# Value products of a decoder layer's attention: one product per key block over up to 384 queries, from transposed probabilities kept for a whole group

## The chip, the cores and the metric

The kernel runs on one core of one Trainium2 chip. The metric is device time in microseconds for one execution of the whole layer; the time before is the median of three runs.

## The reference

One layer of a decoder for 512 positions of width 1024, one batch. After a modulated RMSNorm and one input projection there are two head groups, each of 8 heads of 64 that share 2 key-value heads (below: g = 0, 1; r = 0..3 counts the heads within one g). Group A is sliding-window attention; group B adds three branches, each weighted by a gate:

```python
# A: 128-query blocks, window 128: each block sees its own and the previous key block
o_a = banded_gqa(qa, ka, v_a, 128, rel_bias[:, :8], sinks)
# B: compressed (31 key blocks), selected (here all 8 blocks of 64 fit top-16), window 512
p_c = masked_softmax(q @ k_cmp, c_end <= t);   o_cmp = p_c @ v_cmp
p_s = masked_softmax(q @ k_sel + bias, s <= t); o_sel = p_s @ v_sel
o_win = banded_gqa(qb, k_win, v_win, 512, bias_b, None)
o_b = gb[0] * o_cmp + gb[1] * o_sel + gb[2] * o_win
y = concat(o_a * silu(z_a), o_b * silu(z_b));  out = x + gate * (y @ w_out)
```

With 512 positions, the selected and the window branch are both full causal attention with their own keys and values.

## The kernel before

All matrix products of weights run three times in a split form (a high and a low part of each fp32 number); they stand at L293/L294 (first projection), L484 (`unit_nat`) and L494 (`unit_col`). The attention products on transposed probabilities run in plain fp32.

The attention is cut into slots. A slot is (kind, r, br, i): head r of both g, branch br, query block i of 128. For kind "a" there are 16 slots, each with one or two key blocks. For kind "b" each r has seven: (3, 0), which does query block 0 of both token branches at once, then (1, 1..3) for the selected branch and (2, 1..3) for the window branch, with i + 1 key blocks. `run` (L985) is a pipeline written by hand: in step t it transposes slot t-2, scales slot t-1, computes the scores of slot t, and after the last query block of a group computes the value products of all the slots of that group. Between these it advances a stream (`gen12`) of projection work by an estimated number of microseconds (`per`). A scheduler then orders the instructions of each engine by these priorities and its own estimates; `block()` keeps the TensorE instructions of scores, transposes and value products in their written order, but lets other TensorE work stand between them.

`slot_trans` (L932) transposes the probabilities `pp`/`pa` on TensorE into a PSUM tile `pt`, and ScalarE copies that, query order reversed, to an SBUF tile `ptT` (L942 for one or two key blocks, L952 once per g for three or four). `slot_pv` (L956) multiplies: for one slot, one key block and one g, a stationary 128x64 block of values (`va`, `vs`, `vw`) and a moving 128x128 block of `ptT`, into the 64 rows of g in the PSUM tile `po`. So a head has 14 products in group A, 22 in the selected branch (with 2 + 2 for query block 0) and 18 in the window branch. After the window branch two more products (L974) add the compressed branch from `vc`, of which the 32 rows of r are used, and `PTc`. Then `make_y` (L825) multiplies `po` by the SiLU gate and splits it into `yh` and `yl` for the output projection. The pool `t2` has 38 tiles of 128x512, 16 of which hold `hh` and `hl`, the split input of all projections.

Of the kernel before, what the change touches and what calls it, by code (L numbers as in the profile page):

```python
# [9 lines left out]
F32 = mybir.dt.float32  # L10
# [18 lines left out]
NT2 = 38  # L29
# [52 lines left out]
def hybrid_layer_kernel(ctx, tc, A, out):  # L82
# [42 lines left out]
    hh = [T2(F32R, f"hh{k}") for k in range(8)]  # L125
    hl = [T2(F32R, f"hl{k}") for k in range(8)]
# [485 lines left out]
    def cmp_mlp():  # L612
# [38 lines left out]
        for g in range(2):  # L651
            vc[g] = mp.tile([128, HD], F32, name=f"vc{g}")
            ACT.activation(vc[g], pv[:, 64 * g:64 * g + 64], AF.Copy)
# [278 lines left out]
    def slot_trans(sl):  # L932
        kind, r, br, i = sl["id"]
        P, w = sl["P"], sl["w"]
        nb = w // 128
        if nb <= 2:
            T = T2(F32, "ptT").rearrange("p (g b q) -> p g b q", g=2, b=2)
            pt = PT()
            for g in range(2):
                for b in range(nb):  # L940
                    PE.transpose(pt[:, (nb * g + b) * 128:(nb * g + b + 1) * 128], P[:, g, b * 128:(b + 1) * 128], ident)  # L941
            ACT.copy(T[:, :, 0:nb, :], rev(pt[:, 0:2 * nb * 128].rearrange("p (g b q) -> p g b q", g=2, b=nb)))  # L942
            sl["T"] = [T[:, g] for g in range(2)]
        else:
            sl["T"] = []
            for g in range(2):
                T = T2(F32, "ptT").rearrange("p (b q) -> p b q", b=4)
                sl["T"].append(T)
                pt = PT()
                for b in range(nb):  # L950
                    PE.transpose(pt[:, b * 128:(b + 1) * 128], P[:, g, b * 128:(b + 1) * 128], ident)  # L951
                ACT.copy(T[:, 0:nb, :], rev(pt[:, 0:nb * 128].rearrange("p (b q) -> p b q", b=nb)))  # L952
# [3 lines left out]
    def slot_pv(sl):  # L956
        kind, r, br, i = sl["id"]
# [3 lines left out]
        v = (va, vs, vw, None)[br]  # L961
        nb, j0 = sl["w"] // 128, sl["lo"] // 128
        last = kind == "a"
        first_of = kind == "a" or br == 3
        for b in range(nb):
            for g in range(2):
                vb = (vs, vw)[b][:, 0] if br == 3 else v[:, j0 + b]
                PE.matmul(o[64 * g:64 * g + 64, 128 * i:128 * i + 128], vb[:, 64 * g:64 * g + 64],  # L968
                          sl["T"][g][:, b, :], start=first_of and b == 0, stop=last and b == nb - 1,
                          skip_group_check=True)  # L970
        if i == NB - 1 and br in (0, 2):
            if kind == "b":
                for g in range(2):
                    PE.matmul(o[64 * g:64 * g + 64, :], vc[g][32 * r:32 * r + 32, :],  # L974
                              PTc[g][32 * r:32 * r + 32, :], start=False, stop=True, skip_group_check=True)
# [9 lines left out]
    def run(slots, stream):  # L985

        n = len(slots)
        group = []
        for t in range(n + 3):
            per = PER_A if t < 16 else PER_B[t - 16 >= PER_B[2]]  # L990
            if t < n:
                kind, r, br, i = slots[t]["id"]
                if kind == "a" and i == 0 and r >= 2:
                    load_bias_b(r - 2)
            if 0 <= t - 2 < n:
# [7 lines left out]
            stream.adv(per / 2)  # L1003
            if 0 <= t - 3 < n:
                group.append(slots[t - 3])
                kind, r, br, i = slots[t - 3]["id"]
                if i == NB - 1:
                    with block():
                        for sl in group:
                            slot_pv(sl)  # L1010
                    group = []
                    if kind == "b" and br == 2 and r + 2 < 4:
                        load_bias_b(r + 2)
            stream.adv(per / 2)
# [106 lines left out]
```

## Time and profile before

| | |
|---|---|
| time, median of 3 runs | 313.88 us (313.81 to 314.51) |
| the profiled execution's own time | 314.01 us |
| its span, first to last instruction | 312.2 us |
| TensorE matmuls busy | 304.6 us (98%) |
| VectorE / ScalarE busy | 237.0 us (76%) / 196.9 us (63%) |
| value products at L968, with L974 | 30.2 us of TensorE |
| granted TensorE clock | 1.00 throughout |

Each engine runs its own queue in order, and "busy" is the union of the durations of its instructions. Matmuls overlap each other in time, so what a matmul costs is read from the distance between starts, not from its duration. Each fp32 product of the program appears as two matmul records: 18 products of the window branch are a timeline row "x36".

### The profile page before, as it was taken

To read this page: it belongs to the slowest core of one execution; us is meant where nothing else is said; L and a number is where in the kernel's file an instruction comes from. 1 tells how busy PE (TensorE), PEld (TensorE's weight loads), DVE (VectorE), ACT (ScalarE), POOL (GpSimd) and SP (SyncE) were. 2 spreads that over 40 slices of the span, in tenths; PEclk is the share of its full clock that TensorE was granted. 3 is DMA by queue.
4 is the path that set the end of the run, shared out by engine and by line. 5 is a ranking of instruction groups with operands and counts; after the bars stand their busy time and mean duration, and the time that the engine had idled before them with its cause. 6 is when DMAs were issued, how large, how long until landed. Compare 5 with 4: busy or idle time off the path is not lost.

```text
span 312.2 us, 5975 instructions
## 1 busy us (share of the span) xinstructions
PE 304.6 (98%) x2175; PEld 255.7 (82%) x2175; DVE 237.0 (76%) x668; ACT 196.9 (63%) x477; POOL 4.9 (2%) x21
## 2 busy tenths in 40 slices
PE   8899999999999999999999999999999999999995
PEld 4577778889989889999976887888788788788885
DVE  4779998999896378886989899898678787645221
ACT  5765467677877575978958757877577586502200
POOL 1000000000000000000000000000000000000000
PEclk9999999999999999999999999999999999999999
DMA  7999969623250591141132440337003031352301
GB/s 286 377 398 309 417 217 284 172 87 122 70 156 16 166 347 63 35 136 34 37 134 63 128 181 2 127 90 258 2 0 136 0 138 67 103 202 93 110 34 67
DMA packets 27420, 44.21 MB, mean 142 GB/s; under 512 B 1712, under 2 KB 19408, under 8 KB 27392
## 3 DMA queue, kind: packets, MB, share of 16 engines
q1 hardware_dynamic: 27392, 43.84, 42.0%
q8 instruction: 17, 0.28, 0.4%
q14 instruction: 11, 0.09, 0.1%
HBM read 41.70 MB, written 2.14 MB: 140 GB/s over the span
## 4 chain that ended last, share of the span: by engine, by line
PE 85%; DVE 9%; DMA 2%; ACT 1%; issue 1%; SPq 0%; DVEq 0%
PE pj L494 30%; PE pj L484 10%; PE s L893 8%; PE sq L293 8%; PE po L968 7%; PE pt L951 4%; PE pt L941 4%; PE skv L294 4%; DVE wl L176 2%; PE s L620 2%; DMA xf<-in_xn 2%; PE pt L541 1%; PE po L974 1%; DVE qn L532 1%; DVE qc L536 1%
## 5 line engine op out<-in xcount | busy, mean ns | idle before, releaser
L175 ACT ACTIVATE wh<-raw 128x512 fp32r<-128x512 f32 (+1 forms) x52 | 31.2, 630 | 27.8 <-PE pj L494 27.7
L176 DVE TENSOR_TENSOR wl<-raw,wh 128x512 fp32r<-128x512 f32 (+1 forms) x52 | 35.1, 692 | 7.4 <-ACT wh L175 5.6
L484 PE MATMUL pj<-wh,hl 128*128 128x256 f32 (+1 forms) x128 | 36.9, 288 | 0.0
L484 PE MATMUL pj<-wh,hh 128*128 128x256 f32 (+1 forms) x128 | 36.8, 289 | 0.0
L484 PE MATMUL pj<-wl,hh 128*128 128x256 f32 (+1 forms) x128 | 36.5, 286 | 0.2
L905 ACT ACTIVATE pp<-pp,nm 128x256 f32<-128x256 f32 (+2 forms) x48 | 29.2, 610 | 6.3 <-DVE nm L898 6.2
L494 PE MATMUL pj<-hh,wh 128*128 128x512 f32 x80 | 32.8, 410 | 0.0
L494 PE MATMUL pj<-hl,wh 128*128 128x512 f32 x80 | 31.8, 397 | 0.0
L494 PE MATMUL pj<-hh,wl 128*128 128x512 f32 x80 | 31.7, 397 | 0.0
L898 DVE CUSTOM_DVE_ANT_0 pp<-s,bias 128x256 f32<-128x256 f32 (+2 forms) x48 | 25.4, 550 | 4.9 <-PE s L893 4.8
L494 PE MATMUL pj<-yl,wh 128*128 128x512 f32 (+1 forms) x72 | 26.7, 370 | 0.0
L494 PE MATMUL pj<-yh,wl 128*128 128x512 f32 (+1 forms) x72 | 26.6, 370 | 0.0
L494 PE MATMUL pj<-yh,wh 128*128 128x512 f32 (+1 forms) x72 | 26.3, 370 | 0.0
L484 PEld LDWEIGHTS pj<-wl,hh 128*128 128x128 f32 x128 | 24.1, 189 | 0.7 <-DVE wl L176 0.7
L484 PEld LDWEIGHTS pj<-wh,hl 128*128 128x128 f32 x128 | 24.1, 188 | 0.2 <-issue 0.2
L484 PEld LDWEIGHTS pj<-wh,hh 128*128 128x128 f32 x128 | 24.0, 188 | 0.0
L1047 DVE SCALAR_TENSOR_TENSOR fin<-pj,gate,xr 128x512 f32<-128x512 f32 (+1 forms) x9 | 6.2, 692 | 22.7 <-PE pj L494 22.7
L893 PE MATMUL s<-kTb,qs 128*128 128x256 f32 (+2 forms) x96 | 23.0, 358 | 0.0
L926 DVE TENSOR_SCALAR pp<-pp,rr,grev 128x256 f32<-128x256 f32 (+2 forms) x48 | 21.1, 474 | 0.4
L898 DVE CUSTOM_DVE_ANT_0 pa<-s,bias,nsink 128x256 f32<-128x256 f32 (+1 forms) x32 | 14.3, 449 | 9.4 <-PE s L893 8.4
L952 ACT COPY ptT<-pt 128x384 f32<-128x384 f32 (+1 forms) x32 | 15.7, 531 | 6.3 <-PE pt L951 5.1
L942 ACT COPY ptT<-pt 128x512 f32<-128x512 f32 (+1 forms) x28 | 15.4, 550 | 6.2 <-PE pt L941 6.0
(249 smaller groups left out, 718.8 us busy)
## 6 DMA issues: line engine op xcount, KB each, us to landing
ada_ring<-in_w_ada_ss SPq DMA_DIRECT2D x16, 512.0 KB, 8.7
raw<-in_w_cmp SPq DMA_DIRECT2D x8, 512.0 KB, 4.7
raw<-in_w_gate SPq DMA_DIRECT2D x8, 512.0 KB, 4.1
raw<-in_w_o SPq DMA_DIRECT2D x8, 512.0 KB, 5.2
wst_ring<-in_w_qkv_a SPq DMA_DIRECT2D x8, 384.0 KB, 9.3
bias<-line_d SPq DMA_DIRECT2D x8, 256.0 KB, 4.3
raw<-in_w_q_b SPq DMA_DIRECT2D x4, 512.0 KB, 5.9
raw<-in_w_z_a SPq DMA_DIRECT2D x4, 512.0 KB, 7.5
```

The source lines that it names most:

```text
L175: ACT.activation(wh, src, AF.Copy)
L176: DVE.tensor_tensor(wl, src, wh.bitcast(F32), op=OP.subtract)
L293: PE.matmul(pj_q[tb], lt, w[:, 0:512], start=f, stop=l, skip_group_check=True)
L484: PE.matmul(bank[:, t * n:(t + 1) * n], h[:, tb * 128:(tb + 1) * 128], w[:, k % 2, :], start=k == 0 and m == 0, stop=k == 7 and m == 2)
L494: PE.matmul(bank, w, h[:, cols], start=k == 0 and m == 0, stop=k == 7 and m == 2)
L893: PE.matmul(ps, qs[h][:, 128 * i:128 * i + 128], k[:, hl_, lo:lo + n], start=hl_ == 0, stop=hl_ == 1)
L898: DVE.tensor_tensor_reduce(out=P[:, g, 0:w], in0=ps[:, 0:w], in1=bt, scale=1.0, scalar=init, op0=OP.add, op1=OP.min, accum_out=nm[:, g:g + 1])
L905: ACT.activation(P[:, g, 0:e], P[:, g, 0:e], AF.Exp, bias=nm[:, g:g + 1], scale=-1.0, accum_out=dn[:, g:g + 1])
L926: DVE.tensor_scalar(v, v, rr[:, g:g + 1], gates[:, g, br:br + 1], op0=OP.mult, op1=OP.mult)
L942: ACT.copy(T[:, :, 0:nb, :], rev(pt[:, 0:2 * nb * 128].rearrange("p (g b q) -> p g b q", g=2, b=nb)))
L952: ACT.copy(T[:, 0:nb, :], rev(pt[:, 0:nb * 128].rearrange("p (b q) -> p b q", b=nb)))
L968: PE.matmul(o[64 * g:64 * g + 64, 128 * i:128 * i + 128], vb[:, 64 * g:64 * g + 64], sl["T"][g][:, b, :], start=first_of and b == 0, stop= ...
```

## The change

Three edits belong together.

The transposed probabilities of a whole group stay in one tile: `TTb` (128 keys x 2 g x 4 key blocks x 384 queries) for kind "b", and `TT0`/`TT1` (seven blocks of 128) in turn for kind "a". Query block 0 of kind "b" stays in its own `ptT`. `slot_trans` copies into the right part.

`group_pv` takes the place of `slot_pv`. It goes by key block j: for kind "b" the queries from max(128, 128 j) to 512, so 384, 384, 256 and 128 columns; for kind "a" 256, 256, 256 and 128. A head has 8 products in group A and 10 in each branch of group B. `run` now calls it at the beginning of a step, ahead of the next slot's transposes and scores, where before it stood after them and half of the stream's share. The load of the bias for head r + 2 moves with it.

The compressed values `vc` become a tile of 128 rows x 4 x 64, zero except for rows 32 r to 32 r + 32 of column block r, filled by two memsets on GpSimd and eight copies on ScalarE in place of two; the product uses all 128 rows of `vc` and `PTc`.

To make room, `hh` and `hl` move from `t2` into two tiles of eight parts, and `t2` has 22 tiles.

```diff
-NT2 = 38
+NT2 = 22
...
-    hh = [T2(F32R, f"hh{k}") for k in range(8)]
-    hl = [T2(F32R, f"hl{k}") for k in range(8)]
+    hhl = [con.tile([128, 8, S], F32R, name=name) for name in ("hh", "hl")]
+    hh, hl = ([t[:, k] for k in range(8)] for t in hhl)
...
-            vc[g] = mp.tile([128, HD], F32, name=f"vc{g}")
-            ACT.activation(vc[g], pv[:, 64 * g:64 * g + 64], AF.Copy)
+            vc[g] = mp.tile([128, 4, HD], F32, name=f"vc{g}")
+            POOL.memset(vc[g], 0.0)
+            for r in range(4):
+                own = slice(32 * r, 32 * r + 32)
+                ACT.activation(vc[g][own, r, :], pv[own, 64 * g:64 * g + 64], AF.Copy)
...
+        if br == 3:
+            T = zeroth[r] = T2(F32, "ptT").rearrange("p (g b q) -> p g b q", g=2, b=2)
+        elif kind == "a":
+            T = turned(kind, r, br)[:, :, i + sl["lo"] // 128:][:, :, 0:nb]
+        else:
+            T = turned(kind, r, br)[:, :, 0:nb, 128 * i - 128:128 * i]
...
+    def turned(kind, r, br):
+        key = "b" if kind == "b" else r % 2
+        if key not in TT:
+            TT[key] = mp.tile([128, 2, NB, 384] if kind == "b" else [128, 2, 7, 128], F32, name=f"TT{key}")
+        return TT[key]
...
+    def group_pv(kind, r, br):
...
+        if kind == "a":
+            for j in range(NB):
+                nq = min(2, NB - j)
+                todo.append((j, 128 * j, 128 * nq, [T[:, g, 2 * j:2 * j + nq] for g in range(2)], j == 0, j == NB - 1))
+        else:
+            todo.append((0, 0, 128, [zeroth[r][:, g, br - 1] for g in range(2)], br == 1, False))
+            for j in range(NB):
+                q0 = max(128, 128 * j)
+                todo.append((j, q0, S - q0, [T[:, g, j, q0 - 128:384] for g in range(2)], False, False))
+        for j, q0, n, src, begin, end in todo:
             for g in range(2):
-                vb = (vs, vw)[b][:, 0] if br == 3 else v[:, j0 + b]
-                PE.matmul(o[64 * g:64 * g + 64, 128 * i:128 * i + 128], vb[:, 64 * g:64 * g + 64],
-                          sl["T"][g][:, b, :], start=first_of and b == 0, stop=last and b == nb - 1,
+                PE.matmul(o[64 * g:64 * g + 64, q0:q0 + n], v[:, j, 64 * g:64 * g + 64], src[g], start=begin, stop=end,
                           skip_group_check=True)
...
-                    PE.matmul(o[64 * g:64 * g + 64, :], vc[g][32 * r:32 * r + 32, :],
-                              PTc[g][32 * r:32 * r + 32, :], start=False, stop=True, skip_group_check=True)
+                    PE.matmul(o[64 * g:64 * g + 64, :], vc[g][:, r, :], PTc[g], start=False, stop=True,
+                              skip_group_check=True)
...
+            if 0 <= t - 3 < n:
+                kind, r, br, i = slots[t - 3]["id"]
+                if i == NB - 1:
+                    with block():
+                        group_pv(kind, r, br)
+                    if kind == "b" and br == 2 and r + 2 < 4:
+                        load_bias_b(r + 2)
             if 0 <= t - 2 < n:
...
-            stream.adv(per / 2)
-            if 0 <= t - 3 < n:
-                group.append(slots[t - 3])
...
-                            slot_pv(sl)
...
-            stream.adv(per / 2)
+            stream.adv(per)
```

TensorE, the value products of head r = 1 of group A, first before and then changed (`va`: values; `pa`: probabilities; `csh`, `csT`, `csTv`: the small network that makes the compressed keys and values; `kT`, `qs`: keys and queries of the scores; `wh`, `wl`, `hh`, `hl`: projections):

```order
L893 MATMUL s<-kT_672,qs_892 128x256 x2
L968 MATMUL po<-ptT,va 64x128 x14
L941 MATMUL pt<-first,pa 128x128 x4
L893 MATMUL s<-kT_670,qs_876 128x256 x2
L762 MATMUL pt<-gsig,rest 128x96
```

```order
L896 MATMUL s<-kT_658,qs_878 128x256 x2
L988 MATMUL po<-TT_1182,va 64x256
L634 MATMUL pt<-first,csh 128x128 x2
L988 MATMUL po<-TT_1182,va 64x256 x4
L645 MATMUL s<-rest,csT 64x64 x2
L988 MATMUL po<-TT_1182,va 64x256
L988 MATMUL po<-TT_1182,va 64x128
L649 MATMUL s<-rest,csTv 128x64
L988 MATMUL po<-TT_1182,va 64x128
L484 MATMUL pj<-wh,hh 128x280
L649 MATMUL s<-rest,csTv 128x64 x3
```

One unbroken run of products has become three pieces with transposes and 128-column products of the small network between them.

TensorE, the selected branch of head r = 1 of group B, before and then changed (`pp`: probabilities; L951 and L955 are the transposes of slots with three or four key blocks):

```order
L951 MATMUL pt<-first,pp 128x128 x4
L893 MATMUL s<-kTb_671,qs_1953 128x384 x2
L893 MATMUL s<-kTb_673,qs_1967 128x384 x2
L941 MATMUL pt<-first,pp 128x128 x4
L494 MATMUL pj<-hh_79,wh 128x512
L893 MATMUL s<-kTb_671,qs_1953 128x512 x2
L893 MATMUL s<-kTb_673,qs_1967 128x512 x2
L494 MATMUL pj<-hl_87,wh 128x512
L494 MATMUL pj<-hh_79,wl 128x512
L968 MATMUL po<-ptT,vs 64x128 x2
L968 MATMUL po<-ptT,vw 64x128 x2
L968 MATMUL po<-ptT,vs 64x128 x18
```

```order
L955 MATMUL pt<-first,pp 128x128 x8
L896 MATMUL s<-kTb_657,qs_1917 128x384 x2
L896 MATMUL s<-kTb_659,qs_1931 128x384 x2
L988 MATMUL po<-ptT,vs 64x128 x2
L494 MATMUL pj<-hh,wl 128x512
L988 MATMUL po<-TTb,vs 64x384 x4
L988 MATMUL po<-TTb,vs 64x256 x2
L988 MATMUL po<-TTb,vs 64x128 x2
L949 MATMUL pt<-first,pp 128x128 x4
L896 MATMUL s<-kTb_657,qs_1917 128x512 x2
L896 MATMUL s<-kTb_659,qs_1931 128x512 x2
```

The products now stand four scores behind the group's last transposes; before, four transposes, eight scores and three projection matmuls lay between.

TensorE at the end of the attention, head r = 3, window branch, before and then changed (`yh`, `yl`: the output projection's input; `ptc`, `vc`: the compressed branch):

```order
L951 MATMUL pt<-first,pp 128x128 x6
L494 MATMUL pj<-yh_2659,wl 128x512
L951 MATMUL pt<-first,pp 128x128 x8
L968 MATMUL po<-ptT,vw 64x128 x18
L974 MATMUL po<-ptc_2580,vc_1452 64x512
L974 MATMUL po<-ptc_2590,vc_1454 64x512
```

```order
L955 MATMUL pt<-first,pp 128x128 x4
L494 MATMUL pj<-yh_2586,wh 128x512
L494 MATMUL pj<-yl_2587,wh 128x512
L955 MATMUL pt<-first,pp 128x128 x4
L988 MATMUL po<-ptT,vw 64x128 x2
L988 MATMUL po<-TTb,vw 64x384 x4
L988 MATMUL po<-TTb,vw 64x256 x2
L988 MATMUL po<-TTb,vw 64x128 x2
L993 MATMUL po<-ptc_2515,vc_1426 64x512
L993 MATMUL po<-ptc_2525,vc_1432 64x512
```

The products follow the last transposes at once in both; before they began with the two earlier query blocks, now the third product already reads all three.

More of the change, by code (lines that the diff above doesn't have):

```diff
@@ L941, in slot_trans @@
                     PE.transpose(pt[:, (nb * g + b) * 128:(nb * g + b + 1) * 128], P[:, g, b * 128:(b + 1) * 128], ident)
-            ACT.copy(T[:, :, 0:nb, :], rev(pt[:, 0:2 * nb * 128].rearrange("p (g b q) -> p g b q", g=2, b=nb)))
-            sl["T"] = [T[:, g] for g in range(2)]
+            ACT.copy(T, rev(pt[:, 0:2 * nb * 128].rearrange("p (g b q) -> p g b q", g=2, b=nb)))
         else:
-            sl["T"] = []
             for g in range(2):
-                T = T2(F32, "ptT").rearrange("p (b q) -> p b q", b=4)
-                sl["T"].append(T)
                 pt = PT()
@@ L951, in slot_trans @@
                     PE.transpose(pt[:, b * 128:(b + 1) * 128], P[:, g, b * 128:(b + 1) * 128], ident)
-                ACT.copy(T[:, 0:nb, :], rev(pt[:, 0:nb * 128].rearrange("p (b q) -> p b q", b=nb)))
+                ACT.copy(T[:, g], rev(pt[:, 0:nb * 128].rearrange("p (b q) -> p b q", b=nb)))
+    TT, zeroth = {}, {}
+    def turned(kind, r, br):
[3 more added lines that the diff above has]
+        return TT[key]
     po = {}
-    def slot_pv(sl):
-        kind, r, br, i = sl["id"]
+    def group_pv(kind, r, br):
         if (kind, r) not in po:
@@ L960, in slot_pv @@
         o = po[kind, r]
[L961 to L965, printed above, removed]
+        v = (va, vs, vw)[br]
+        T = turned(kind, r, br)
+        todo = []
+        if kind == "a":
[8 more added lines that the diff above has]
+        for j, q0, n, src, begin, end in todo:
             for g in range(2):
[L967 to L969 removed]
+                PE.matmul(o[64 * g:64 * g + 64, q0:q0 + n], v[:, j, 64 * g:64 * g + 64], src[g], start=begin, stop=end,
                           skip_group_check=True)
[L971 removed]
+        if br in (0, 2):
             if kind == "b":
                 for g in range(2):
[L974 to L975 removed]
+                    PE.matmul(o[64 * g:64 * g + 64, :], vc[g][:, r, :], PTc[g], start=False, stop=True,
+                              skip_group_check=True)
             if kind == "a":
@@ L987, in run @@
         n = len(slots)
-        group = []
         for t in range(n + 3):
```

8 lines of the change are left out of this document (removed).

## The prediction

> **What bounds the kernel now.** I read the page first: busy time per engine, the granted clock and the chain that ended last.
>
> ```profile
> PE 304.6 (98%) x2175; PEld 255.7 (82%) x2175; DVE 237.0 (76%) x668; ACT 196.9 (63%) x477; POOL 4.9 (2%) x21
> PEclk9999999999999999999999999999999999999999
> PE 85%; DVE 9%; DMA 2%; ACT 1%; issue 1%; SPq 0%; DVEq 0%
> ```
>
> TensorE is busy 98% of the span, at the higher clock level in every slice, and 85% of the chain is its own. So time goes where TensorE's queue spends it: a matmul's price is the distance from its start to the next start, and a wait at its head is paid in full, since everything behind stands still.
>
> Next I asked for the value products' share (windows, tile `po` alone).
>
> ```profile
> 102.00:160.00 58.00, 6.94 (x112) 6.12 (x112) 0.00 (x0) 1.76 (x3) 1.00 0.39 123
> 160.00:266.00 106.00, 23.04 (x336) 18.08 (x336) 0.69 (x1) 1.79 (x3) 1.00 0.28 90
> ```
>
> Some 30 us of TensorE, in 448 records. Whether fewer and wider products shrink that depends on what a narrow one pays beyond its columns. Two neighbours in the timeline of TensorE tell, both with a stationary of 128x64 and alternating halves of the array; the last line is the chain's piece for the second of them.
>
> ```profile
> 98.73 3.74 PE L620 MATMUL s<-raw,pp 128*64 128x256 f32 x32
> 102.30 1.70 PE L968 MATMUL po<-ptT,va 128*64 128x128 f32 x28
> 103.93 0.66 PE L941 MATMUL pt<-first,pa 128*128 128x128 f32 x4
> 104.34 0.48 PE L893 MATMUL s<-kT,qs 128*128 128x256 f32 x2
> 102.47 1.53 PE po L968 x28
> ```
>
> A record of 128 columns costs 1.53 / 28 = 0.0546 us. A record of 256 columns costs at most (102.30 - 98.73) / 32 = 0.1116 us, its slow first one included; two narrow ones cost 0.1092. Cost is linear in columns here. 1.63 us pass until the transposes start, so leaving the 64-column shape of the array costs 0.10 us.
>
> **The change, part by part.**
>
> *A, wider products.* The columns stay the same (9 blocks per branch before, 384 + 384 + 256 + 128 now). Products fall from 4 x 14 + 8 x 20 = 216 to 4 x 8 + 8 x 10 = 112, so 208 records fewer. The fixed part of a record lies between nothing and, allowing the rows 0.0025 us of reading error, 0.0025: a gain between 0 and 0.5 us. I take 0.25, in the middle.
>
> The Trainium skill ("TensorE: Matmul & The Clock Gate", section "Back-to-back issue gap") gives a sustained 81 ns per matmul at 128 columns and 131 ns at 512, so a wide column would cost 0.4 of a narrow one. By that, with an estimate of 114 ns at 384, the products of 128 columns would lose about 0.44 of their 432 x 0.0546 = 23.6 us, and the sum would be near 304 us. The rows here differ: twice the columns took 2.04 times as long, not 1.2.
>
> For the other prices I read the end of the attention.
>
> ```profile
> 195.31 1.17 PE L893 MATMUL s<-kTb,qs 128*128 128x512 f32 x4
> 196.33 0.39 PE L494 MATMUL pj<-hh,wl 128*128 128x512 f32 x1
> ...
> 257.16 1.17 PE L893 MATMUL s<-kTb,qs 128*128 128x512 f32 x4
> 258.26 0.44 PE L968 MATMUL po<-ptT,vs 128*64 128x128 f32 x4
> 258.53 0.39 PE L968 MATMUL po<-ptT,vw 128*64 128x128 f32 x4
> 258.75 2.13 PE L968 MATMUL po<-ptT,vs 128*64 128x128 f32 x36
> 260.81 0.50 PE L494 MATMUL pj<-yl,wh 128*128 128x512 f32 x1
> 261.15 0.82 PE L951 MATMUL pt<-first,pp 128*128 128x128 f32 x6
> ...
> 262.04 1.05 PE L951 MATMUL pt<-first,pp 128*128 128x128 f32 x8
> 263.02 2.19 PE L968 MATMUL po<-ptT,vw 128*64 128x128 f32 x36
> 265.14 1.07 PE L974 MATMUL po<-ptc,vc 32*64 32x512 f32 x4
> 266.14 0.50 PE L494 MATMUL pj<-yh,wh 128*128 128x512 f32 x1
> 266.48 0.40 PE L494 MATMUL pj<-yl,wh 128*128 128x512 f32 x1
> 266.71 0.40 PE L494 MATMUL pj<-yh,wl 128*128 128x512 f32 x1
> ```
>
> *B, 128 rows of `vc`.* Four records of 512 columns cost 4 x 4 x 0.0546 = 0.87 us by columns; L974 takes 1.00 (265.14 to 266.14). The 36 records before it take 2.12, where 36 x 0.0546 = 1.97: again an exit of 0.10 and a slow first record. Row count is not in the price: the 0.87 is that of 128-row records. With one shape for all, one exit goes, and the 0.03 by which L974 exceeds columns and exit: 0.13 us, four times: 0.5 us gained. Bounds: 0.4 (the exit alone) and 0.6 (with a slow first record of 0.05, as 258.26 to 258.53 against 258.53 to 258.75).
>
> *C, stretches in the 64-column shape.* The order has 14 stretches before and 18 now: the products of r = 0 of group A left the small network's neighbourhood, those of r = 1 are in three pieces, and two branches of group B (r = 0 window, r = 1 selected) in two each; a separate one of the network went. A stretch costs on entry 0.08 (257.16 to 258.26 is 1.10; the same four scores took 1.02 from 195.31), 0.05 in its first record and 0.10 on exit: 0.23 us. The first matmul behind it pays once more: a projection 0.11 (260.81 to 261.15 is 0.34, against 0.23 from 266.48), four transposes 0.05 (103.93 to 104.34 is 0.41; the four below 0.36).
>
> ```profile
> 203.49 0.60 PE L941 MATMUL pt<-first,pp 128*128 128x128 f32 x4
> 203.85 0.48 PE L494 MATMUL pj<-hh,wh 128*128 128x512 f32 x1
> ```
>
> Before, ten stretches end at projections and four at transposes: 1.30 us; now five and thirteen: 1.20. So C is 4 x 0.23 - 0.10 = 0.8 us lost. Bounds 0.4 (two of the pieces close up) to 1.4 (all new ends at projections).
>
> *D, waits for the last copy.* Before, the products went slot by slot, so the last query block's copies were needed by the last 8 of 18. Now the first key block already reads all query blocks. At the end of the attention the eight transposes start at 262.04, and the copies run on ScalarE:
>
> ```profile
> 255.45 1.05 ACT L952 COPY ptT<-pt 128x512 f32<-128x512 f32 x2
> 261.68 2.08 ACT L952 COPY ptT<-pt 128x384 f32<-128x384 f32 x4 [1.52 <-PE pt L951]
> ```
>
> They end at 261.68 + 2.08 = 263.76, when the products had run since 263.02 on older copies. In the new order two products of query block 0 cover 0.27 us; the third waits until 263.76: 0.47 us. In two more places almost as little lies between the last transposes and the products: the selected branch of r = 1 (four scores of 384, two products, one projection matmul) and of r = 3 (four scores, two products). For the latter, before, the transposes had started at 253.48 and given way to scores at 254.27; the copies ended at 256.50, 2.2 us later, since softmax work stood ahead of them on ScalarE.
>
> ```profile
> 253.48 1.03 PE L951 MATMUL pt<-first,pp 128*128 128x128 f32 x8
> 254.27 0.94 PE L893 MATMUL s<-kTb,qs 128*128 128x384 f32 x4
> ```
>
> Scores (0.94) and two products (0.27) cover 1.2 of that, and the new order puts three projection matmuls more (0.7) ahead of these transposes, which leaves 0.3. For r = 1 the exponentials of the slot between stand ahead of the copies, against the same cover and one projection matmul. I take the one wait that rows give whole, 0.5 us, in each of three places: 1.5 in all. Bounds: 0 if ScalarE is early, and 3.5 if these two places wait 1.2 each and the end 1.1, where the transposes themselves also stand behind exponentials queued after a copy. Behind a waiting product stand the next slot's transposes and scores, and behind those VectorE and ScalarE: they only catch up.
>
> *E, costs I put at nothing.*
>
> ```profile
> 117.79 0.34 ACT L653 ACTIVATE vc<-s 128x64 f32<-128x64 f32 x2 [0.76 <-PE s L649]
> 120.54 0.37 ACT L942 COPY ptT<-pt 128x256 f32<-128x256 f32 x1 [2.40 <-PE pt L941]
> L305 POOL MEMSET raw<- 128x672 f32 x1 | 0.7, 657 | 0.3 <-POOLq L1111 0.3
> bias<-line_d SPq DMA_DIRECT2D x8, 256.0 KB, 4.3
> ```
>
> Eight copies into `vc` in place of two: 8 x 0.17 = 1.4 us, 1.0 more, ahead of 2.40 idle; without that cover the next softmax is up to 1.0 late. The memsets (two of 256 columns, 0.5 us by the 672-column row) stand at the head of GpSimd's queue, long before the copies. The bias loads leave SP's queue in the same step as before, now behind two gate loads that stood behind them; landing takes 4.3 us, and the first reader is a whole head later. The copies' rows of 384 are shown by no row; the elements are the same, and I bound it by the two copy rows of 128x512 above, 0.5 each, at nothing. `hh` and `hl` change address alone; TensorE's order is the same up to the first value product.
>
> **The sum**, on the profiled execution: 314.01 - 0.25 - 0.5 + 0.8 + 1.5 = 315.56 us. The median of the runs is 0.13 below that execution: 315.4 us.
>
> **Rivals.** *Faster, by waits that go.* TensorE waits some 2.3 us in eight places between 86 and 161 us, mostly for VectorE. First, longest and last:
>
> ```profile
> 85.63 0.29 PE L484 MATMUL pj<-wh,hh 128*128 128x280 f32 x1
> 86.03 0.40 PE L484 MATMUL pj<-wl,hh 128*128 128x280 f32 x1
> 130.51 0.28 PE L484 MATMUL pj<-wh,hl 128*128 128x256 f32 x1
> 131.21 0.51 PE L893 MATMUL s<-kT,qs 128*128 128x256 f32 x2 [0.43 <-DVE nm L898]
> 160.25 0.40 PE L494 MATMUL pj<-hl,wh 128*128 128x512 f32 x1
> 160.69 0.54 PE L541 MATMUL pt<-ident_r,qc 128*128 128x128 f32 x4
> ```
>
> (0.40 against 0.13, 0.70 against 0.12, 0.44 against 0.23.) The order of that part is new. If these waits go and D is nothing, 314.01 + 0.05 - 2.3 - 0.13 = 311.6. It decides for faster once 1.0 us of them goes and none comes. Against it: the order there is new by small shifts only. *Same: the copies are early.* D is nothing and A to C cancel: 313.9. For it: TensorE's queue is paced by the stream, and ScalarE is 63% busy. *Fixed cost per record*: if half of 0.0546 were fixed, 208 x 0.027 = 5.7 us would go: 314.01 - 5.7 + 0.3 - 0.13 = 308.5. The 256-column row speaks against it. The section named above is this rival's rule. *Slower still*: all eight branches of group B wait 0.5: 317.9.
>
> **How the numbers follow.** The likeliest case, three waits, has 0.50, its own range 314.9 to 317.2 (D from 0.8 to 3). Same 0.27, waits gone 0.15, fixed cost 0.03, all branches waiting 0.05. The range for 8 in 10 reaches down into the waits that go, and up to D's upper end: 312.4 to 317.4. A measurement of this kernel tells 0.3%, or 0.94 us, from no change. Faster holds the third and fourth case, 0.18; same 0.27; slower 0.55.
>
> **What would show it.** Products of 384 columns: a record at about 0.165 us between starts (A). No 32-row records, and `po` one shape to its end (B). Entries to the 64-column shape paid at the pieces (C). At the selected branches of r = 1 and 3 and the last window branch, a gap of 0.3 to 1.2 us on TensorE before the first 384-column product, ended by a copy on ScalarE (D). The prediction fails if these gaps are absent, if the waits between 86 and 161 us are gone, or if a 384-column record costs clearly less than three narrow ones.

## The result

The changed kernel takes 318.67 us (median, 318.19 to 319.26) against 313.98 us: a ratio of 1.0145, interval 1.0129 to 1.0160. The forecast was 315.4 us, with a range of 312.4 to 317.4. Slower was right; the loss is 4.7 us and not 1.5.

The profiled execution took 319.26 us with a span of 317.1. So 2.16 us lie outside the span, where 1.81 did before (314.01 less 312.2): 0.35 us of the loss are in no row of the profile.

First the page (busy time, then the chain):

```profile
PE 307.8 (97%) x1967; PEld 250.9 (79%) x1967; DVE 238.2 (75%) x668; ACT 199.3 (63%) x483; POOL 5.1 (2%) x23
PE 80%; DMA 8%; DVE 6%; ACT 3%; SPq 1%; issue 1%; DVEq 0%
```

208 matmul records fewer, and TensorE is busy 3.2 us longer. Next the windows view, tile `po` alone (columns: window, its length, busy and records of PE, PEld, DVE, ACT, then clock, DMA share and rate); first the kernel before, then the changed one:

```profile
92.00:160.00 68.00, 6.94 (x112) 6.12 (x112) 0.00 (x0) 1.76 (x3) 1.00 0.36 116
160.00:276.00 116.00, 23.25 (x336) 18.08 (x336) 1.38 (x2) 1.79 (x3) 1.00 0.28 92
```

```profile
92.00:160.00 68.00, 7.85 (x64) 4.41 (x64) 0.00 (x0) 2.38 (x4) 1.00 0.39 120
160.00:276.00 116.00, 25.09 (x176) 14.91 (x176) 1.39 (x2) 1.20 (x2) 1.00 0.28 94
```

The products cost more in both groups, with half the records. To see where, I measured each branch from the start of its first product to the start of the instruction behind its last, less what matmuls of other jobs took in between. In us:

| branch | before | changed |
|---|---|---|
| group A, r = 0, 1, 2, 3 | 1.63, 1.68, 1.68, 1.68 | 1.66, 2.26, 1.67, 1.66 |
| B selected, r = 0, 1, 2, 3 | 2.55 each | 2.31, 2.66, 2.31, 2.92 |
| B window with `vc`, r = 0, 1, 2, 3 | 3.12 each | 3.95, 3.28, 3.28, 3.69 |
| sum | 29.35 | 31.65 |

(Half of query block 0, 0.22 us, moved from the selected branch to the window branch.) The head r = 2 of group B, which is disturbed least, takes 2.31 + 3.28 = 5.59 us against 5.67. Five entries stand well above their neighbours: r = 1 of group A, the selected branches of r = 1 and 3, the window branches of r = 0 and 3. Here are the two of r = 3 behind an undisturbed selected branch, in TensorE's timeline of the changed kernel (start, duration, then the instructions):

```profile
234.97 0.44 PE L988 MATMUL po<-ptT,vs 128*64 128x128 f32 x4
235.24 2.11 PE L988 MATMUL po<-TTb,vs 128*64 128x384 f32 x16
237.28 0.33 PE L949 MATMUL pt<-first,pp 128*128 128x128 f32 x1
...
259.75 0.44 PE L988 MATMUL po<-ptT,vs 128*64 128x128 f32 x4
260.09 2.64 PE L988 MATMUL po<-TTb,vs 128*64 128x384 f32 x16
262.67 0.55 PE L949 MATMUL pt<-first,pp 128*128 128x128 f32 x3
...
269.92 0.44 PE L988 MATMUL po<-ptT,vw 128*64 128x128 f32 x4
270.19 2.20 PE L988 MATMUL po<-TTb,vw 128*64 128x384 f32 x13
...
273.61 0.50 PE L494 MATMUL pj<-yh,wl 128*128 128x512 f32 x1
```

The selected branch of r = 2 takes 2.04 us for its 16 records (235.24 to 237.28), that of r = 3 2.58 (260.09 to 262.67). ScalarE's timeline has the copies they read:

```profile
259.46 1.06 ACT L956 COPY TTb<-pt 128x512 f32<-128x512 f32 x2
...
269.03 0.59 ACT L956 COPY TTb<-pt 128x512 f32<-128x512 f32 x1 [0.71 <-PE pt L955]
270.03 0.58 ACT L956 COPY TTb<-pt 128x512 f32<-128x512 f32 x1 [0.41 <-PE pt L955]
```

The last copies end at 260.52 and 270.61 us, after the first 384-column product has begun. One copy is done per g, and each g has its own half of the array. Around the first 384-column record of the same three branches the timeline shows:

```profile
235.24 0.49 PE L988 MATMUL po<-TTb,vs 128*64 128x384 f32 x2
...
260.09 0.54 PE L988 MATMUL po<-TTb,vs 128*64 128x384 f32 x1
...
270.19 0.49 PE L988 MATMUL po<-TTb,vw 128*64 128x384 f32 x1
```

In the undisturbed branch two records, one of each g, start together, and the next two 0.32 us later. In the others g = 0 goes ahead alone; the first record of g = 1 starts 0.05 us after its copy has ended (at 260.58 and 270.67 us). From there both halves work side by side, a record every 0.32 us in each, but g = 1 stays up to half a microsecond behind to the end of the branch, and the branch is longer by about that lag. The window branch of r = 0 is cut by transposes of another job as well:

```profile
195.16 0.44 PE L988 MATMUL po<-ptT,vw 128*64 128x128 f32 x4
195.43 0.81 PE L988 MATMUL po<-TTb,vw 128*64 128x384 f32 x2
196.16 0.66 PE L716 MATMUL pt<-first,pa 128*128 128x128 f32 x4
196.75 1.72 PE L988 MATMUL po<-TTb,vw 128*64 128x384 f32 x11
...
199.69 0.55 PE L949 MATMUL pt<-first,pp 128*128 128x128 f32 x3
```

From 195.43 to 196.16 the two records of one product, that of g = 0, take 0.73 us alone in their half; that of g = 1 comes behind the transposes. Undisturbed, two records, one in each half, take 0.32.

The other large piece is not a product at all. The waits of TensorE from 80 to 275 us, before and then changed:

```profile
PE s L893 <- DVE nm L898: 0.4, 1, 0.4
PE pt L541 <- DVE qc L536: 0.2, 1, 0.2
```

```profile
PE pt L667 <- DVE kcn L663: 1.1, 1, 1.1
```

This transpose of the small network's keys (`kcn`) stands still for 1.09 us. The timelines of TensorE, VectorE and ScalarE there:

```profile
121.17 0.24 PE L667 MATMUL pt<-first,kcn 64*128 64x64 f32 x1 [1.09 <-DVE kcn L663]
```

```profile
119.16 0.69 DVE L176 TENSOR_TENSOR wl<-raw,wh 128x512 fp32r<-128x512 f32 x1 [1.43 <-ACT wh L175]
...
120.59 0.18 DVE L800 TENSOR_TENSOR gsig<-pj,rest 128x24 f32<-128x24 f32 x1 [0.67 <-ACT vw L799]
120.69 0.33 DVE L663 SCALAR_TENSOR_TENSOR kcn<-s,n_y,rest 64x128 f32<-64x128 f32 x1
```

```profile
117.80 0.67 ACT L656 ACTIVATE vc<-s 32x64 f32<-32x64 f32 x3 [0.34 <-PE s L649]
118.49 0.63 ACT L175 ACTIVATE wh<-raw 128x512 fp32r<-128x512 f32 x1
119.15 1.12 ACT L656 ACTIVATE vc<-s 32x64 f32<-32x64 f32 x5
120.28 0.28 ACT L799 ACTIVATE vw<-pj 128x128 f32<-128x128 f32 x1
```

Read backwards: `kcn` stands behind a gate sum that waited 0.67 us for the copy of `vw`, which stood behind five copies into `vc`; ahead of it VectorE had waited 1.43 us for a weight's high part, which stood behind the first three. Both waits are ended by an engine that was copying `vc`: 1.79 us (0.67 + 1.12), which the forecast had at 1.4 us of ScalarE and at no cost in time.

### The profile page after: what moved, and what is told of

It reads as the page before. It is cut to its first block, busy times and chain, and to the rows that moved or that the text cites. A ratio compares the mean times of both kernels' runs of the same rounds, so it can differ in the third digit from the quotient of the medians.

```text
span 317.1 us, 5550 instructions
## 1 busy us (share of the span) xinstructions
PE 307.8 (97%) x1967; PEld 250.9 (79%) x1967; DVE 238.2 (75%) x668; ACT 199.3 (63%) x483; POOL 5.1 (2%) x23
## 3 DMA queue, kind: packets, MB, share of 16 engines
HBM read 41.70 MB, written 2.14 MB: 138 GB/s over the span
## 4 chain that ended last, share of the span: by engine, by line
PE 80%; DMA 8%; DVE 6%; ACT 3%; SPq 1%; issue 1%; DVEq 0%
PE pj L494 31%; PE po L988 9%; PE pj L484 8%; PE s L896 8%; PE sq L293 5%; DMA ada_ring<-in_w_ada_ss 5%; PE pt L955 4%; PE pt L949 4%; DMA wst_ring<-in_w_qkv_a 3%; PE skv L294 2%; PE s L620 2%; PE po L993 1%; DVE wl L176 1%; PE pt L541 1%; DVE kT L570 1%
## 5 line engine op out<-in xcount | busy, mean ns | idle before, releaser
L175 ACT ACTIVATE wh<-raw 128x512 fp32r<-128x512 f32 (+1 forms) x52 | 32.1, 632 | 32.9 <-PE pj L494 32.8
L494 PE MATMUL pj<-hh,wh 128*128 128x512 f32 x80 | 31.9, 399 | 0.0
L956 ACT COPY TTb<-pt 128x384 f32<-128x384 f32 (+1 forms) x32 | 15.8, 525 | 4.4 <-PE pt L955 4.4
L908 ACT ACTIVATE pa<-pa,nm 128x257 f32<-128x257 f32 (+1 forms) x32 | 15.4, 482 | 4.4 <-DVE nm L901 3.5
```

Of the source, the lines that this page charges most:

```text
L175: ACT.activation(wh, src, AF.Copy)
L494: PE.matmul(bank, w, h[:, cols], start=k == 0 and m == 0, stop=k == 7 and m == 2)
L908: ACT.activation(P[:, g, 0:e], P[:, g, 0:e], AF.Exp, bias=nm[:, g:g + 1], scale=-1.0, accum_out=dn[:, g:g + 1])
L956: ACT.copy(T[:, g], rev(pt[:, 0:nb * 128].rearrange("p (b q) -> p b q", b=nb)))
```

## The experiments

Theory P: the loss is waits for the last copies and cuts in the products, made by the early place. Theory K: the eight copies into `vc` hold up `kcn`. Theory S1 and S2: a late start of the first projection in the changed kernel's profile is due to the change, or to the execution. Ratios are to the kernel before, timed with them on the same chip (314.1 to 314.4 us).

| run | median us | ratio, 95% interval |
|---|---|---|
| again (the changed kernel) | 318.59 | 1.0143 (1.0130 to 1.0157) |
| e1_pad | 314.49 | 1.0013 (1.0003 to 1.0022) |
| e2_hhl | 314.82 | 1.0030 (1.0017 to 1.0043) |
| e3_mask | 317.06 | 1.0095 (1.0081 to 1.0108) |
| e4_q3 | 316.29 | 1.0068 (1.0055 to 1.0082) |
| e6_late | 315.13 | 1.0024 (1.0014 to 1.0034) |
| e9_b_mask | 315.21 | 1.0033 (1.0022 to 1.0045) |
| e8_late_mask | 315.55 | 1.0042 (1.0029 to 1.0054) |
| e10_four | 319.15 | 1.0152 (1.0131 to 1.0174) |
| e11_q3_four | 316.47 | 1.0077 (1.0055 to 1.0098) |
| e12_late_four | 314.83 | 1.0019 (1.0006 to 1.0033) |
| e13_b_four | 314.01 | 0.9997 (0.9986 to 1.0009) |
| e7_q3_mask | 315.85 | 1.0046 (1.0033 to 1.0060) |
| e16_late_four_t2 | 314.24 | 0.9996 (0.9986 to 1.0006) |

**again**: no edit.

> The changed kernel as it stands, once more, for a second profile. In the first one, all of TensorE's work from the first projection on stood 1.07 us later than in the kernel before: a transpose waited for the load of x until 9.97 instead of 9.13 us, and the first projection began at 15.97 instead of 14.89. Theory S1: the change causes this (the addresses of hh and hl, or the two memsets of vc on GpSimd); then the first projection starts at 15.7 to 16.2 us here too. Theory S2: such a delay differs from execution to execution; then it starts anywhere from 14.8 on, and the span follows it. Both expect a median of 318.3 to 319.0 us.

TensorE's timeline at the start, of the kernel before, the changed one, and the changed one again (the load that a transpose waits for, the first `mod_pe` product, the first projection):

```profile
9.13 0.63 PE L324 MATMUL sq<-first,xf 128*128 128x128 f32 x4 [0.69 <-DMA xf<-in_xn]
11.81 1.07 PE L223 MATMUL pj<-ada_ring,scz 128*32 128x256 f32 x16
14.89 0.50 PE L293 MATMUL sq<-swh,hh 128*128 128x512 f32 x1 [0.41 <-ACT hh L389]
```

```profile
9.97 0.63 PE L324 MATMUL sq<-first,xf 128*128 128x128 f32 x4 [0.93 <-DMA xf<-in_xn]
12.65 0.64 PE L223 MATMUL pj<-ada_ring,scz 128*32 128x256 f32 x8
15.97 0.50 PE L293 MATMUL sq<-swh,hh 128*128 128x512 f32 x1 [0.58 <-ACT hh L389]
```

```profile
8.97 0.63 PE L324 MATMUL sq<-first,xf 128*128 128x128 f32 x4 [0.68 <-DMA xf<-in_xn]
11.65 1.07 PE L223 MATMUL pj<-ada_ring,scz 128*32 128x256 f32 x16
14.97 0.50 PE L293 MATMUL sq<-swh,hh 128*128 128x512 f32 x1 [0.58 <-ACT hh L389]
```

S2: the same program waits for the load until 9.97 us in one execution and 8.97 in another. Comparing the first pair of profiles alone, I would have put 1.0 us on the change that isn't its own. One part is the change's: from the first `mod_pe` product to the projection it is 3.32 us, before 3.08, in both executions. The wait of 1.1 us for `kcn` and the branches of products repeat within 0.03 us.

**e1_pad**: the padding alone, in the kernel before.

```diff
-NT2 = 38
+NT2 = 37
...
-            vc[g] = mp.tile([128, HD], F32, name=f"vc{g}")
-            ACT.activation(vc[g], pv[:, 64 * g:64 * g + 64], AF.Copy)
+            vc[g] = mp.tile([128, 4, HD], F32, name=f"vc{g}")
+            POOL.memset(vc[g], 0.0)
+            for r in range(4):
+                own = slice(32 * r, 32 * r + 32)
+                ACT.activation(vc[g][own, r, :], pv[own, 64 * g:64 * g + 64], AF.Copy)
...
-                    PE.matmul(o[64 * g:64 * g + 64, :], vc[g][32 * r:32 * r + 32, :],
-                              PTc[g][32 * r:32 * r + 32, :], start=False, stop=True, skip_group_check=True)
+                    PE.matmul(o[64 * g:64 * g + 64, :], vc[g][:, r, :], PTc[g], start=False, stop=True,
+                              skip_group_check=True)
```

> The kernel before with the zero-padded vc alone (memsets, eight copies of 32 rows, products on 128 rows; one T2 buffer fewer, for room). By the recorded term B: 4 x 0.13 = 0.5 us gained, the copies free: 313.5 us. Theory K (the eight copies stand in ScalarE's queue ahead of work that TensorE comes to wait for; in the changed kernel they ran from 117.80 to 120.04 us and a wait of 1.26 us ended at 121.17): the window branches show only 0.06 less each (0.35 us above their columns before, 0.29 in the changed kernel), 0.24 in all, and somewhere between 118 and 125 us TensorE waits 0.5 to 1.3 us more than before: 314.2 to 315.0 us.

The windows view (`po`) and ScalarE's copies:

```profile
160.00:276.00 116.00, 22.67 (x336) 18.18 (x336) 1.38 (x2) 1.79 (x3) 1.00 0.28 92
```

```profile
118.58 1.80 ACT L656 ACTIVATE vc<-s 32x64 f32<-32x64 f32 x8 [0.77 <-PE s L649]
```

The products gave 23.25 - 22.67 = 0.58 us: term B was right (0.5), and theory K's 0.24 was not. The copies take 1.8 us, and nobody waits for `kcn`, since here neither a weight copy nor that of `vw` stands among or behind them. Yet the median rose by 0.4, into theory K's range but not by its wait: 2.15 us lie outside the span (1.78 before), and the median span, 312.3, stayed what it was. In the profiled execution the first projection starts at 15.60 us instead of 14.89, which hides the gain there; whether the padding causes that, or the execution as in "again", and what takes the 0.58 us in the median, is not shown.

**e2_hhl**: the move of `hh` and `hl` alone, in the kernel before.

```diff
-NT2 = 38
+NT2 = 22
...
-    hh = [T2(F32R, f"hh{k}") for k in range(8)]
-    hl = [T2(F32R, f"hl{k}") for k in range(8)]
+    hhl = [con.tile([128, 8, S], F32R, name=name) for name in ("hh", "hl")]
+    hh, hl = ([t[:, k] for k in range(8)] for t in hhl)
```

> The kernel before with hh and hl as two tiles outside the T2 pool, and T2 at 22 buffers: that part of the change alone. Theory S1 by the addresses: the first projection begins near 15.9 us and the time is 315.0 us. Theory S2, and the recorded prediction, which put this part at nothing: 313.9 us, within 0.4.

0.7 us slower than the kernel before, as neither theory has it. The first projection again comes 3.31 us after the first `mod_pe` product (0.23 lost, 0.1 of it won back by its end). The order of the later work differs too, and the profile, of the slowest execution (316.38 us), has a new wait:

```profile
PE pt L941 <- DVE pp L926: 0.5, 1, 0.5
```

Which of the two, addresses or fewer buffers, is not separated.

**e3_mask**: the changed kernel, `vc` by VectorE.

```diff
+    own = con.tile([128, 4], F32, name="own")
+    POOL.memset(own, 0.0)
+    for r in range(4):
+        POOL.memset(own[32 * r:32 * r + 32, r:r + 1], 1.0)
...
-            POOL.memset(vc[g], 0.0)
-            for r in range(4):
-                own = slice(32 * r, 32 * r + 32)
-                ACT.activation(vc[g][own, r, :], pv[own, 64 * g:64 * g + 64], AF.Copy)
+            DVE.tensor_tensor(vc[g], pv[:, None, 64 * g:64 * g + 64].to_broadcast([128, 4, HD]),
+                              own[:, :, None].to_broadcast([128, 4, HD]), op=OP.mult)
```

> The changed kernel, with the padded vc made by one VectorE product per half (the 128x64 result, broadcast over four heads, times a 0/1 mask of four columns that GpSimd writes at the start), in place of two memsets and eight ScalarE copies. In this version the selected branch of r = 1 also stands in one piece, which should give 0.2 us. Theory K: the 1.26 us wait of the transpose of kcn goes, VectorE pays two products of some 0.35 us instead: 317.0 to 317.5 us. Rival: that wait comes from VectorE's own order (a weight's low part and a gate sum stand ahead of kcn), and stays: 318.3 to 318.7 us.

1.5 us faster than the changed kernel, as theory K says. TensorE at the transpose of `kcn`, which now waits for nothing by name:

```profile
120.05 0.28 PE L488 MATMUL pj<-wl,hh 128*128 128x256 f32 x1
120.39 0.24 PE L669 MATMUL pt<-first,kcn 64*128 64x64 f32 x1
```

0.34 us between the starts, against 1.37 (119.80 to 121.17). The weight's low part and the gate sum still stand ahead of `kcn` on VectorE: the rival falls.

**e4_q3**: the changed kernel, the last query block apart.

```diff
-            for j in range(NB):
+            for j in range(NB - 1):
                 q0 = max(128, 128 * j)
-                todo.append((j, q0, S - q0, [T[:, g, j, q0 - 128:384] for g in range(2)], False, False))
+                todo.append((j, q0, 384 - q0, [T[:, g, j, q0 - 128:256] for g in range(2)], False, False))
+            for j in range(NB):
+                todo.append((j, 384, 128, [T[:, g, j, 256:384] for g in range(2)], False, False))
```

> The changed kernel with the last query block apart: per branch of group B the products over query blocks 1 and 2 of all key blocks come first, those over query block 3 (the last copies) last; the columns stay the same, the widest product is 256. In this order every branch of group B also stands in one piece. In the changed kernel's two profiles the stretches of products stand above their columns by 0.18 us in a selected branch that neither waits nor is cut, by 0.29 in such a window branch, but by 0.80 and 0.70 in the two of r = 3, by 0.53 in the selected one of r = 1 and by 0.97 in the window one of r = 0. Theory D (waits for the last copies, and cuts): these excesses go, 0.62 + 0.41 + 0.35 + 0.68 = 2.05 us: 316.5 us. Rival: the copies are later than the 0.6 us that the other query blocks cover, and only the cuts close: 317.5 us. Second rival: the wide records themselves are dear, and nothing goes: 318.5 us.

2.3 us faster than the changed kernel; theory D (the part of theory P that this edit tests) had said 2.05. All selected branches take 2.32 us and all window branches 3.18, with 96 records more (the windows view):

```profile
160.00:276.00 116.00, 22.59 (x272) 15.78 (x272) 1.38 (x2) 1.19 (x2) 1.00 0.29 94
```

So the waits and cuts of group B cost 24.4 - 22.0 = 2.4 us by branches and 2.3 by the clock, and the wide records themselves bring 0.02 us per branch over these narrower ones (2.31 against 2.32). The run does not part the waits from the cuts, since no job cuts a branch in its order; by the table the waits are 1.55 us and the cuts 0.9. The 1.1 us for `kcn` are still there.

**e6_late**: products at the old place, behind the scores and half the stream, with one gathering tile per branch.

```diff
-        key = "b" if kind == "b" else r % 2
+        key = f"b{br}" if kind == "b" else r % 2
...
-            if 0 <= t - 3 < n:
-                kind, r, br, i = slots[t - 3]["id"]
-                if i == NB - 1:
-                    with block():
-                        group_pv(kind, r, br)
...
-            stream.adv(per)
+            stream.adv(per / 2)
+            if 0 <= t - 3 < n:
+                kind, r, br, i = slots[t - 3]["id"]
+                if i == NB - 1:
+                    with block():
+                        group_pv(kind, r, br)
...
+            stream.adv(per / 2)
```

> The changed kernel with its products at the place of the kernel before (behind the next transposes, the scores and half of the stream's share), and the gathered probabilities of the two branches in two tiles instead of one, since the next branch's copies now come before the products. Theory P (the early place costs: waits for copies, cuts, and the wait for kcn, as ScalarE's copies of vc meet a weight copy only in the early order): stretches fall to 0.18 and 0.29 us above their columns everywhere, 2.65 us in all, and the 1.26 us of kcn go: 314.7 us. Rival G (gathering into one tile with strided copies, or the wide products, cost as well): 316 us or more. If the 22 buffers of T2 cost what they did in the kernel before with hh and hl moved (0.7 us), 315.4.

315.13 us, 3.5 below the changed kernel and between theory P's two figures; rival G falls. The place carries most of the loss. No transpose waits for `kcn`, and by the measure of the table the branches take 28.7 us, against 29.35 before:

```profile
92.00:160.00 68.00, 6.88 (x64) 4.31 (x64) 0.00 (x0) 1.77 (x3) 1.00 0.39 121
160.00:276.00 116.00, 22.69 (x176) 11.08 (x176) 1.38 (x2) 1.79 (x3) 1.00 0.28 90
```

**e9_b_mask, e8_late_mask**: `vc` by the masked VectorE products of e3, in the kernel before and in the late version; VectorE writes the mask too.

```diff
+    own = con.tile([128, 4], F32, name="own")
+    DVE.memset(own, 0.0)
+    for r in range(4):
+        DVE.memset(own[32 * r:32 * r + 32, r:r + 1], 1.0)
...
+            DVE.tensor_tensor(vc[g], pv[:, None, 64 * g:64 * g + 64].to_broadcast([128, 4, HD]),
+                              own[:, :, None].to_broadcast([128, 4, HD]), op=OP.mult)
```

> The kernel before with the padded vc alone, made by two VectorE products with a 0/1 mask that VectorE writes at the start; neither ScalarE nor GpSimd does anything for it. In the run with the padding by copies each window branch took 2.97 us in place of 3.12, 0.6 in all, but the time between span and execution was 2.15 us instead of 1.8, and the median rose by 0.4. Theory O1 (the 0.35 us outside the span come with GpSimd's memsets or ScalarE's extra copies): outside 1.8, time 313.5 us. Theory O2 (they come with the padded tile however it is made): outside 2.15, time 313.9 us. Rival: the two products (0.35 us each) delay VectorE at the small network and give back the gain: 314.1 us or more.

> Both: products at the place of the kernel before, two gathering tiles, and the padded vc by two masked VectorE products. By theory P and the masked vc without cost outside the span: 0.35 us below the run with the late place alone, 314.3 us. It would beat the kernel before only if the wide products give their 0.03 us in each of twelve stretches and the padding its 0.6: 313.2 us.

Neither theory holds: e9 came out as its rival has it, and e8 above both of its figures. The products of e9 took 22.66 us, the gain of e1 again, and the time outside the span was 1.78, but the span grew by 1.0 us. Two more products on VectorE stand ahead of `kcn`, whose transpose starts at 120.57 us instead of 119.86. But TensorE does not wait for it, and the longest wait for `nm` is only 0.2 us longer (0.6 instead of 0.4), so what the rest of the 1.0 us is stays open. In e8 the mask cost 0.4 us against e6. Outside its span lay 2.14 us, without any memset on GpSimd: O1 falls as well, and so does O2, since e9 has the padded tile and 1.78.

**e10_four, e11_q3_four, e12_late_four, e13_b_four**: four copies into `vc` instead of eight, in four kernels.

```diff
...
+        vcs = mp.tile([128, 2, 4, HD], F32, name="vc")
+        POOL.memset(vcs, 0.0)
+        for r in range(4):
+            own = slice(32 * r, 32 * r + 32)
+            ACT.activation(vcs[own, :, r, :], pv[own, 0:128].rearrange("p (g d) -> p g d", g=2), AF.Copy)
+        for g in range(2):
+            vc[g] = vcs[:, g]
```

> The changed kernel with four ScalarE copies into vc in place of eight (both halves in one tile, one copy of 32 rows and 2x64 columns per head) and one memset; the order of the engines stays what it was, with the weight copy behind the second of four copies in place of the third of eight. The copies started 0.227 us apart. Theory K: 4 x 0.227 = 0.9 us less stand ahead of the copy of vw, for which VectorE waits ahead of kcn; the 1.26 us wait falls to about 0.35: 317.7 us. Rival (VectorE's order alone, the copies do not matter): the wait stays, 318.6 us.

> The last query block apart and the four copies together. Theory D and theory K act in different places, so their gains add: 316.3 - 0.9 = 315.4 us. If the wait for kcn were made up later by waits that shrink, less than 0.9: 315.7 to 316.3.

> Products at the place of the kernel before, two gathering tiles, and four copies into vc. In that order no transpose waited for kcn with eight copies either. Theory K (the copies cost only where the weight copy and kcn stand behind them): no gain, 315.1 us. Rival (ScalarE's time costs everywhere): 0.9 less, 314.2 us, level with the kernel before.

> The kernel before with the padded vc alone, by four copies in place of eight. With eight: 314.5 us, the window branches 0.6 us shorter in all, the time outside the span 0.35 longer. Theory K: nothing waited for the copies there, so 314.5 us again. If the copies did delay something unseen by up to 0.9 us, 313.6 to 314.2, and the kernel before would be beaten.

In e10 theory K's mechanism holds and its time does not. The four copies took 1.10 us instead of 1.79, and the wait for `kcn` fell by the same 0.69, to 0.40 us:

```profile
118.33 0.55 ACT L655 ACTIVATE vc<-s 32x128 f32<-32x128 f32 x2 [0.34 <-PE s L649]
...
119.56 0.55 ACT L655 ACTIVATE vc<-s 32x128 f32<-32x128 f32 x2
```

```profile
PE s L620 <- DMA raw<-in_w_cmp: 0.4, 1, 0.4
PE pt L668 <- DVE kcn L664: 0.4, 1, 0.4
```

But a product of the small network now waited for its weights, ten us earlier and with no part in the edit, and the time did not fall: the ratio is 1.0152, that of "again" 1.0143, and the intervals overlap. e11 shows the same wait (0.2) and stayed at e4's time, above both of its forecasts. In these two the last load of those weights landed at 109.8 us, in "again" at 107.4; why was not tried. e12 is as theory K says: 0.3 us below e6, within the intervals. e13 is not: theory K expected no change, and it is 0.5 us below e1. So the copies may have delayed something there that no wait names; the two intervals just overlap, so this is not shown. With four copies the padding costs the kernel before nothing, and gives it nothing either.

**e7_q3_mask**: both gains together, the edit of e4 with `vc` and its mask as in e8.

> The changed kernel with the last query block apart and vc by two masked VectorE products (the mask written by VectorE): no copies of vc on ScalarE, no waits for the last copies. Alone, the first gave 318.6 - 316.3 = 2.3 us and the second 318.6 - 317.1 = 1.5. If these two are the loss and add: 314.8 us (in this order the window branch of r = 0 is cut in two again, which may keep 0.3 to 0.5 of it: 315.2). Rival (the time saved early is lost again in later waits, as with four copies): 316 us or more.

315.85 us. The wait for `kcn` is gone, and the window branch of r = 0 is cut again: 4.34 us from its first product to the transposes behind it, 0.59 of them for the four transposes between, so 3.75 where 3.18 is undisturbed. Against e4, 1.03 us are saved on `kcn` and 0.57 are lost there; 0.46 should be left, and 0.44 are by the medians (316.29 to 315.85), 0.7 by the ratios. But the forecast, 315.2 us, was missed: alone the two runs gave 2.3 and 1.5 us, together 2.7, so the gains add only in part, and the part of e3's 1.5 us that is not the wait for `kcn` did not come.

**e16_late_four_t2**: e12 with `hh` and `hl` back in the pool.

```diff
-NT2 = 22
+NT2 = 38
...
-    hhl = [con.tile([128, 8, S], F32R, name=name) for name in ("hh", "hl")]
-    hh, hl = ([t[:, k] for k in range(8)] for t in hhl)
+    hh = [T2(F32R, f"hh{k}") for k in range(8)]
+    hl = [T2(F32R, f"hl{k}") for k in range(8)]
```

> Products at the place of the kernel before, two gathering tiles, four copies into vc, and hh and hl back in the T2 pool (38 buffers). The version with hh and hl outside took 314.8 us. In every version with hh and hl outside the first projection begins 3.31 us after the first mod_pe product, against 3.08 where they are in the pool. Theory H (the move costs 0.2 us there and 0.2 to 0.5 in the later order): 314.1 to 314.6 us. Rival (the move costs nothing): 314.8 us. Below 313.8 it would beat the kernel before, whose stretches of products are 0.66 us longer in all.

314.24 us, 0.6 below e12, as theory H says, and level with the kernel before. It is the second run, after e2, in which the home of `hh` and `hl` is worth 0.6 us or more. With the old place, the old home of `hh` and `hl` and half the copies, the wide products are neither better nor worse than the narrow ones. No version beats the kernel before by more than can be measured.

## Why the prediction was wrong

The forecast lacked 3.2 us of the loss. The step that failed is E, the costs put at nothing; C was too small besides, and a part of the loss lies outside the span.

*The rule that carried it was right.* Cost is linear in columns: group A's branch takes 1.66 us with 16 records and 1.68 with 28. Terms A and B were forecast at 0.75 us; the undisturbed branches gained 2.55 + 3.12 - 2.31 - 3.17 = 0.19 per head, some 0.8 in all, 0.58 of it by the padding. The rule of the Trainium skill ("TensorE: Matmul & The Clock Gate", section "Back-to-back issue gap") would have had nine us go; nothing of that showed. By the Trainium skill's figures, with estimates of 114 ns at 384 columns and 98 ns at 256, 0.38 of the products' 23.6 us would go; the forecast wrote 0.44, and a sum near 304 us where this gives 307.

*D, right in place and near in size.* Forecast 0.5 us in each of three places. They lost 0.35 (selected, r = 1; 0.2 by the wait, the rest by the projection that cuts the branch), 0.61 (selected, r = 3) and 0.52 (last window, to e6's 3.17). The window branches of r = 1 and 2, which I had not counted, wait 0.11 us each: g = 1 starts there at 219.72 and 246.54 us, again 0.05 after its copy. In all 1.55 us for 1.5 forecast, and partly by luck, since the places differ. Nor is it as I had drawn it: the profile has no gap ahead of the 384-column products, but one half of the array that goes ahead and one that lags.

*C, mis-sized by 0.7 us.* Forecast 0.8 for four more stretches. The pieces of r = 1 in group A cost 0.60, the cut in the window branch of r = 0 0.78 with a product that ran alone, and the one in the selected branch of r = 1 0.15: 1.5 us. The small network's matmuls between the pieces (`csh`, `csT`, `csTv`) also took 1.50 us instead of 1.24. I had priced a cut by its entry and exit, and neither by what it does to two products that run side by side nor by what the cutting matmuls pay.

*E is the step that failed.* "Eight copies into `vc` ... ahead of 2.40 idle", at nothing. I had looked at the idle time of ScalarE in the old order, and at the next softmax as the only one to wait. In the new order a weight copy stands among the copies of `vc` and the copy of `vw` behind them, and VectorE queues that weight's low part and a gate sum ahead of `kcn`. TensorE stood still for 1.09 us. Without the copies (e3) this wait is gone, and with half of them (e10) it is shorter by the 0.69 us that they save. `hh` and `hl`, also at nothing, cost 0.23 us at the first projection, and their move with the smaller pool 0.7 us of time in the kernel before (e2).

*What no row holds.* 0.35 us outside the span. It is 1.8 in the kernel before, e2 and e9, and 1.9 to 2.6 in all others but one execution of e3; no single part of the change sets the two sets apart (e8 has no memset on GpSimd and no copies, e1 no gathering tile, and both have 2.15). This stays open.

*The sum*, from the second profile (execution 318.25, span 316.1). Its first projections end at 53.27 us, as in the kernel before: there a load that landed 0.16 us earlier offsets what the move of `hh` and `hl` costs. Behind that the branches of products take 2.3 us more, -0.8 (A, B) + 1.5 (C) + 1.55 (D). The wait for `kcn` adds 1.1, and the waits for `nm` and `qc` that went give back 0.6: TensorE's idle time between 80 and 165 us rises from 0.92 to 1.42 only. The small network's matmuls add 0.3, and 0.37 lie outside the span. That is 3.4 of 4.24 us; the last 0.8 I did not separate. By the clock, each run against the kernel before that was timed with it, the old place (e6) takes back 3.6 of 4.5 us, and the old home of `hh` and `hl` with four copies (e16) the rest.

*The rivals.* None was it. "All eight branches wait 0.5", 317.9 us, was the nearest, for the wrong reason: the selected branches of r = 0 and 2 do not wait at all, and two window branches 0.11 us. Of the waits between 86 and 161 us, those for `nm` and `qc` went, as that rival hoped, and the 1.09 for `kcn` came.

## What to carry to other kernels

Where cost is linear in columns, wider products gain next to nothing (0.02 us in a branch of group A), and gathering moves the first use of the last piece to the front: keep the newest piece apart and multiply it last, which made an undisturbed branch 0.02 us longer and gave 2.3 us here, 0.9 of it through cuts that closed. An edit "covered by idle time" must be priced in the queue of the new order: list what stands behind it on its engine and who waits for that; eight small copies cost 1.1 us through two engines. Before a difference in the start of two profiles is explained, look at a second profile of the same program.

## What the runs showed of the hardware

- With 64-column stationaries of fp32 the two halves of the array worked side by side, each with a 384-column record every 0.32 us (16 records from 235.24 to 237.28 us). When the data of one half came late, the other went ahead and the late half stayed behind to the end: the branch took 2.58 us instead of 2.04, with no idle row on TensorE.
- ScalarE's copies of 32 rows, each to other rows than the last, took 0.21 us and started 0.227 apart; two copies of 128 rows into separate tiles started 0.12 apart before (118 us, the row of 0.34 for two). Four copies of twice the columns started 0.28 apart. For the same elements eight copies took 1.79 us and four 1.10.
- Two executions of one program differed by 1.0 us in when a load of x had landed, and so in the start of all that follows.
